# An x load written earlier, second places for stick-breaking keys and values, one dense place less, and other transfer constants in the planner

## The chip, the cores and the metric

One core of a Trainium2 chip runs the whole layer. The metric is the time of one execution on the device in microseconds (us); the figure for a kernel is the median of several executions.

## What is computed

One decoder layer on x of 2048 tokens by 1024 features: RMSNorm, one projection to queries, keys and values for two groups of heads, the two kinds of attention, an output projection with residual, RMSNorm, an MLP with squared ReLU (1024 to 4096 and back) with residual, and a last RMSNorm. Four heads are differential heads (two softmax maps with a distance bias, the second subtracted with weight lam), eight are stick-breaking heads (weights from a running product of 1 - sigmoid):

```python
def diff_attn_block(q1, q2, k1, k2, v, lam, slopes, q0):
    ...
    a = probs(q1, k1) - lam * probs(q2, k2)
    return jnp.einsum('bhqk,bhkd->bhqd', a.astype(v.dtype), v)

def stick_breaking_block(q, k, v, q0):
    ...
    later = lax.cumsum(log_om, axis=3, reverse=True) - log_om
    w = jnp.where(strict, jnp.exp(log_beta + later), 0.0)
    return jnp.einsum('bhqk,bhkd->bhqd', w.astype(v.dtype), v)

def reference(x, attn_norm, w_in, ...):
    h = x
    for l in range(DEPTH):
        a = rmsnorm(h, attn_norm[l])
        h = h + hybrid_mixer(a, w_in[l], ...)
        m = rmsnorm(h, mlp_norm[l])
        u = jnp.square(jax.nn.relu(jnp.einsum('bsd,df->bsf', m, w_up[l])))
        h = h + jnp.einsum('bsf,fd->bsd', u, w_down[l])
    return rmsnorm(h, final_norm)
```

## The kernel before

**Numbers.** Every float32 operand of a matmul is split into two float32r parts, hi (a rounded copy, made by ScalarE) and lo (the rest, a subtraction). A dense product of one 128-wide output slice for one block of 512 tokens is 24 matmuls: 8 chunks of 128 features times hi*hi, hi*lo and lo*hi.

**Blocks and stages.** The tokens stand in reverse order, in four blocks of 512. Block 3 holds the earliest tokens, so it attends to one chunk of keys and block 0 to four. The dense work runs in this order: the projection (QKV) of blocks 3 and 2 together (`emit_qkv((3, 2), ...)`), QKV of blocks 1 and 0, then for each block from 3 to 0 the output projection (`emit_out`) and the MLP (`emit_mlp`). The first use of a weight loads it raw (`split_w`: one transfer of 512 KB), splits it and stores the parts to DRAM; later uses load the parts. In `split_w` the two lo subtractions of a weight run on GpSimd, each as two instructions of 256 columns.

**Three streams and a planner.** The program writes units of work (one instruction, or up to eight matmuls) into three streams: "dense", "diff" (differential heads) and "sb" (stick-breaking heads). `Plan.order` then simulates the five engines with constants for durations and decides one order for all; the engines execute that order as it stands, each its own instructions in turn, and wait by semaphores. Loads and stores are all issued by SyncE (SP), in that order too. TensorE takes a ready unit of an attention head before one of the dense stream (`key`), so dense work fills what the heads leave. For a transfer the planner reckons with 0.42 us on SP, then bytes at a rate by row length behind the transfers that it already has in flight, and 2.2 us more until the data are there. A dense unit may be at most 100 units (`AHEAD`) ahead of the oldest one that isn't placed.

**Places.** Buffers come from pools of slots ("places"). A tile names a home, and a home may use certain pools; tiles of one home and one stream get their places strictly in the order in which the program writes them (`queue`, by `line`): while the first in the line has not been reached, none behind it gets a place. The pools that matter here: "early" (25 places of 4 KB a partition) in the first QKV; "xp" (24 places) during the whole kernel, of which 17 are for "bx", the normed x of blocks 1 and 0; "late" (24 places) opens when the attention is over; the attention's own pools open when all of "early" is done, with one place for the queries of each kind (`qa`, `sq`), two for `ka` and `v`, and one each for `ska` and `sv`, the keys and values of the stick-breaking heads.

**The start.** The first weight, x of block 3, two more weights, then small constants are loaded; three products of block 3 run, then three of block 2 with the same weights. `load_x(2)` is written after the first product, as step 1 of `emit_qkv`, and `norm_to(2)` (scaling by the gain, split to hi on ScalarE and lo on VectorE) as step 2. The tile `rows` of `space`, in which the rows of 1/rms of blocks 3 and 2 stand, has the home "be", as the x tiles have; it is first written when the rms of block 3 is known (`rms_row`, a ScalarE copy from PSUM). The constants' scratch tile `tmp` is a "be" tile too, with the four lambda vectors loaded into it.

Of the kernel before, what the change touches and what calls it, by code (L numbers as in the profile page):

```python
# [28 lines left out]
P = 128  # L29
S = 2048  # L30
D = 1024
# [75 lines left out]
class Plan:  # L107
# [52 lines left out]
    def duration(self, eng, method, kw, out, ins, u):  # L160
        n = math.prod(out.shape[1:])
        small = [v for v in ins if math.prod(v.shape[1:]) * 4 > n]
        sb = [v for v in small if v.tile.home != "psum"]
        if eng == "PE":
            if kw.get("lhsT", kw.get("in_")).dtype == F32:
                return 0.11 if "in_" in kw else 0.225
            return max(0.06, n * 0.000437 + 0.008)
        if eng == "DVE":
            u.dual = len(sb) > 1
            u.psum = any(v.tile.home == "psum" for v in ins)  # L170
            if method == "tensor_tensor_scan":
                return 0.15 + n * 0.0022
            if method == "tensor_reduce":
                n = math.prod(ins[0].shape[1:])
            if method == "tensor_copy" and sb and n >= 256:
                u.dual = True
                return 0.43
            extra = 0.055 if isinstance(kw.get("scalar"), View) else 0.085 if "accum_out" in kw else 0.0
            return 0.15 + n / 960 + extra
        if eng == "ACT":  # L180
            u.psum = any(v.tile.home == "psum" for v in ins)
            extra = 0.09 if isinstance(kw.get("scale"), View) or isinstance(kw.get("bias"), View) else 0.0
            return 0.18 + (0.0 if u.psum else 0.03) + n / 1200 + extra + (0.19 if "accum_out" in kw else 0.0)
        if eng == "POOL":
            if method == "memset":
                return 0.2 + n / 1000
            if kw.get("op") == ALU.pow:
                return 1.65
            u.dual = True
            if method == "tensor_tensor":  # L190
                return 0.19 + n * (0.00216 if out.dtype == F32R else 0.00165)
            if method == "affine_select":
                return 0.3
            return 0.19 + n * 0.00085
        row = min([out.shape[-1]] + [v.shape[-1] for v in ins])
        u.bytes = math.prod(out.shape) * 4
        u.moves = u.bytes / {P: 265e3, HW: 300e3, BW: 335e3, D: 360e3}.get(row, 200e3)
        return 0.42


    def order(self, slots, phase_of, caps, log=None):
# [101 lines left out]
        while done < len(units):  # L303
# [14 lines left out]
            while progress:  # L318
                progress = False
                for e in avail:  # L320
# [3 lines left out]
                    for u in waiting[e]:  # L324
                        if u.ready > now + 1e-9:
                            continue
                        k = self.key(u, now)
                        if best is not None and k >= best[0]:
                            continue
                        if u.stream == "dense" and u.i > dense[at_dense].i + self.AHEAD:  # L330
                            continue
                        spots, ok = [], True
                        for t in u.allocs:
                            if queue[u.stream, self.line(t)][-1] is not t:
                                ok = False
                                break
                            s = place(t, now)
                            if s is None:
                                ok = False
                                break  # L340
                            spots.append((t, s))
                            if len(u.allocs) > 1:
                                free[s[0]].remove(s[1])
                        if len(u.allocs) > 1:
                            for t, s in spots:
                                free[s[0]].append(s[1])
                        if ok:
                            best = k, u, spots
# [16 lines left out]
                    if e == "SP":  # L365
                        avail[e] = now + u.dur
                        begin = max(now + 0.1, dma_free)
                        dma_free = begin + u.moves
                        finish = begin + 2.2 + u.moves
                    else:  # L370
                        finish = start + u.dur
                        avail[e] = finish
                        if e == "PE":
                            if now > self.pe_end + 0.05:
                                gaps.append((now - self.pe_end, now, u))
                            self.pe_end = finish
# [13 lines left out]
                    for s in u.succ:  # L390
                        s.ndeps -= 1
                        s.ready = max(s.ready, finish if s.eng == e else res + (0.04 if s.eng == "POOL" else 0.0))
                        if not s.ndeps:
                            waiting[s.eng].append(s)
                            heapq.heappush(events, s.ready)
                            if s.eng == "PE":
                                heapq.heappush(events, s.ready + self.MARGIN)
                    for t in users.get(id(u), ()):
                        t.left -= 1
                        for kind in gate.get(t.home, ()):  # L400
# [15 lines left out]
        self.report = dict(end=max(u.finish for u in units), busy=busy, gaps=gaps)  # L416
        return out

    MARGIN, AHEAD, pe_end = 0.4, 100, 0.0

    MOST = {("be", "xp"): 7, ("we", "early"): 8, ("xe", "early"): 4, ("w", "xp"): 6, ("x", "xp"): 2, ("y", "xp"): 6,
            ("wm", "xp"): 4, ("wq", "xp"): 5, ("xm", "xp"): 2, ("ym", "xp"): 6, ("x", "late"): 4, ("w", "late"): 12}
# [9 lines left out]
    def key(self, u, now):  # L432
        if u.eng == "PE":
            late = u.ready + self.MARGIN > now
            return (late, u.stream == "dense", u.frac if u.stream != "dense" else u.n)
        if u.eng == "SP":
            return (u.stream == "dense", u.frac if u.stream != "dense" else u.n)

        return u.ready - (10.0 if u.psum else 0.0)

# [11 lines left out]
def layer_kernel(ctx: ExitStack, tc: tile.TileContext, a: dict, out: bass.AP):  # L452
# [5 lines left out]
    tiny = ctx.enter_context(tc.tile_pool(name="tiny", bufs=1))  # L458


    ATT = dict(qa=1, ka=2, e=12, v=2, ha0=2, ha1=2, fa=3, sq=1, ska=1, sv=1, set=8, ser=2, hb0=2, hb1=2, fb=2, osb=1)
    TINY = dict(rvx=2, rrx=2, rx=4, rvh=2, rrh=2, negm=2, l=2, gam=2, rl=2, mm=2, left=8)
    homes = {"be": ["early", "xp"], "we": ["early"], "ye": ["early"], "xe": ["early"], "e": ["e", "e2"], "bx": ["xp"], "b": ["late", "xp"], "w": ["late", "xp"], "y": ["late", "xp"],
             "x": ["late", "xp"], "wm": ["xp"], "ym": ["m", "xp"], "xm": ["xp"], "yq": ["m", "xp"], "wq": ["xp"]}
    homes.update({k: [k] for k in [*ATT, *TINY] if k not in homes})
    plan = Plan(homes)
# [70 lines left out]
    def split_w(name, *at):  # L537

        tiles = [buf(F32R, kind=1) for _ in range(2)]
        if (name, at) in kept:  # L540
            for t, d in zip(tiles, kept[name, at]):
                dma(t, d)
            return Weights(tiles)
        raw = buf(kind=3)
        dma(raw, a[name][at])
        kept[name, at] = []
        for j, t in enumerate(tiles):
            r, hi, lo = raw[:, j * BW:(j + 1) * BW], t[:, 0:BW], t[:, BW:D]
            act.activation(out=hi, in_=r, func=ACTF.Copy)

            for i in range(0, BW, HW):
                pool.tensor_tensor(out=lo[:, i:i + HW], in0=r[:, i:i + HW], in1=hi[:, i:i + HW].bitcast(F32), op=ALU.subtract)
            kept[name, at].append(dt(f"d_{name}_{'_'.join(map(str, at))}_{j}", [P, D]))
            dma(kept[name, at][j], t)
        return Weights(tiles)
# [9 lines left out]
    def halves(last=False):  # L565
# [1 line left out]
        b_ = [buf(F32R, last) for _ in range(KD)]  # L567
        h = [t.rearrange("p (k s) -> p k s", k=2) for t in b_]
        h = h[0::2], h[1::2]
        return h, ([h[0][k // 2][:, k % 2] for k in range(KD)], [h[1][k // 2][:, k % 2] for k in range(KD)], b_)  # L570

    def x_pair():
        t = buf(F32R, kind=2)
# [9 lines left out]

    def space(last=False):
        n = len(rows) % 2
        rows.append(rows[-1] if n else buf(last=last))
        return halves(last) + (rows[-1][:, n * BW:(n + 1) * BW],)

    rows = []
# [1 line left out]
    def norm_x(xs, where):  # L591

        tiles, views, row = where
        for kp, x in enumerate(xs):
            for k in range(2):
                g = g_attn[:, 2 * kp + k:2 * kp + k + 1]
                x_, hi, lo = x[:, k * BW:(k + 1) * BW], tiles[0][kp][:, k], tiles[1][kp][:, k]
                act.activation(out=hi, in_=x_, func=ACTF.Copy, scale=g)
                vec.scalar_tensor_tensor(out=lo, in0=x_, scalar=g, in1=hi.bitcast(F32), op0=ALU.mult, op1=ALU.subtract)
        return views + ([], lambda: rms(xs, row))  # L600
# [427 lines left out]
    for e in starts[1:]:  # L1028
        ws[e] = [split_w("w_qk", e)]

    nxt = {}

    def load_to(b):
        def f():
# [24 lines left out]
    for i, n in enumerate(("lambda_q1", "lambda_k1", "lambda_q2", "lambda_k2")):  # L1059
# [16 lines left out]
    vec.tensor_scalar(out=neglam, in0=neglam, scalar1=-LAM_INIT, scalar2=None, op0=ALU.add)  # L1076


    emit_qkv((3, 2), xs, 3, {1: load_to(2), 2: norm_to(2, False), 12: load_to(1), 13: norm_to(1, True),
                             16: load_to(0), 18: norm_to(0, True)}, ws)  # L1080
    home[:] = ["b", "wq", "yq", "xm"]
    emit_attention(3)
# [4 lines left out]
    def mlp_of(b, xs):  # L1087
        def early():
# [11 lines left out]
    emit_mlp(0, *emit_out(0, xs), 8, lambda: None)  # L1100


    slots = dict(xp=[f"b{i}" for i in range(24)], early=[f"e{i}" for i in range(25)], late=[f"l{i}" for i in range(24)],
                 psum=[f"p{i}" for i in range(8)])
    slots.update({k: [f"{k}{i}" for i in range(n)] for k, n in [*ATT.items(), *TINY.items()]})
    slots.update(m=["m0", "m1"], e2=[f"f{i}" for i in range(4)])
    phases = {k: ["be", "we", "ye", "xe"] for k in [*ATT, "m"]}
    phases.update(e2=["yq", "ym"], late=list(ATT))

    def caps(kind, plan):  # L1110
# [78 lines left out]
```

## Time and profile before

| what | value |
|---|---|
| median of the runs | 2978.68 us (2973.56 to 2979.01, 3 runs) |
| profiled execution, its own time | 2972.79 us |
| its span, first to last instruction | 2971.0 us |
| TensorE busy | 2892.6 us, 97% |
| VectorE, ScalarE, GpSimd busy | 59%, 39%, 37% |
| mean granted TensorE clock | 0.991 |
| DMA: mean rate, share of the 16 engines | 226 GB/s, 67.5% |

A page of the profile gives one execution. Nearly all instructions carry the line of the helper that issues them (L447), so groups are told apart by tile names: `d` and `dn` are the PSUM tiles of dense products, `s`, `pt`, `od` and `os` those of the attention, `w` a split weight, `x` a raw one, `b` a large dense tile, `y` the tile of an output that is to be stored, names with `d_` DRAM. A wait is put down to the event that came last before the waiting instruction began.

### The profile page before, as it was taken

The page shows a single profiled execution, that of the slowest core. Times are in us where ns is not written, and L with a number is a line of the kernel's source. Part 1 is how long each engine was busy: PE and PEld are TensorE (multiplying, and loading weights), DVE is VectorE, ACT ScalarE, POOL GpSimd, SP SyncE. Part 2 cuts the span into 40 slices and gives each one's busy share as a digit, 9 for nine tenths or more (in the row PEclk, how much of TensorE's full clock was granted, in tenths as well). Part 3 has the DMA queues.
Part 4 walks back from the last instruction along what each step waited for, and adds up shares of the span by engine and source line. Part 5 has one row for each costly group of instructions (what it writes and reads, how often), then busy time and mean ns, then how long its engine had stood idle before and what let it go on. Part 6 is the DMA issues. An engine that isn't in the chain of part 4 may idle for free.

```text
span 2971.0 us, 42391 instructions
## 1 busy us (share of the span) xinstructions
PE 2892.6 (97%) x14928; PEld 2439.6 (82%) x14928; DVE 1767.4 (59%) x3193; ACT 1146.2 (39%) x2390; POOL 1099.7 (37%) x1589
## 2 busy tenths in 40 slices
PE   8999999999999999999999999999999999999997
PEld 6889789888887888788788888888888888888886
DVE  5243477777777888884588888887443333421112
ACT  4232255555655555663355555553120100211101
POOL 3221266554677787775344444543000000000000
PEclk9999999999999999999999999999999999999998
DMA  8776897777887877678866665654865556645551
GB/s 268 246 245 202 259 270 233 218 218 230 264 269 244 262 255 254 238 250 288 308 216 204 198 189 192 215 186 169 325 244 200 183 184 241 255 143 205 205 185 71
DMA packets 304164, 670.51 MB, mean 226 GB/s; under 512 B 26960, under 2 KB 121424, under 8 KB 303952
## 3 DMA queue, kind: packets, MB, share of 16 engines
q1 hardware_dynamic: 303952, 667.80, 67.5%
q8 instruction: 119, 1.95, 0.3%
q14 instruction: 93, 0.76, 0.1%
HBM read 491.53 MB, written 176.16 MB: 225 GB/s over the span
## 4 chain that ended last, share of the span: by engine, by line
PE 88%; DMA 6%; DVE 2%; POOL 1%; issue 1%; ACT 1%; SPq 1%; POOLq 0%; DVEq 0%; ACTq 0%
PE d L447 43%; PE dn L447 23%; PE s L447 8%; PE pt L447 6%; PE os L447 4%; PE od L447 3%; DMA v<-d_dv 2%; DMA sq<-d_sq 1%; DMA b<-x_T 1%; SPq L447 1%; DMA qa<-d_dq 1%; DVE b L447 1%; PE r L447 0%; POOL set L447 0%; POOL w L447 0%
## 5 line engine op out<-in xcount | busy, mean ns | idle before, releaser
L447 PE MATMUL d<-b,w 128*128 128x512 f32 x5376 | 1300.9, 395 | 14.1 <-ACT b L447 11.7
L447 PEld LDWEIGHTS d<-b,w 128*128 128x128 f32 x5376 | 1005.3, 189 | 233.1 <-ACT b L447 12.3
L447 PE MATMUL dn<-y,w 128*128 128x512 f32 x3072 | 742.3, 394 | 1.5 <-DVE y L447 1.4
L447 PEld LDWEIGHTS dn<-y,w 128*128 128x128 f32 x3072 | 572.9, 188 | 129.1 <-DVE y L447 1.7
L447 DVE TENSOR_TENSOR b<-b,dn 128x512 f32<-128x512 f32 x416 | 284.8, 685 | 294.9 <-PE dn L447 289.7
L447 POOL TENSOR_TENSOR w<-x,w 128x256 fp32r<-128x256 f32 x384 | 321.8, 860 | 254.5 <-ACT w L447 190.0
L447 POOL TENSOR_TENSOR set<-ser 128x512 f32<-128x512 f32 (+2 forms) x320 | 308.4, 965 | 153.3 <-DVE ser L447 139.7
L447 POOL TENSOR_TENSOR rrx<-rvx,mhalf 128x4 f32<-128x4 f32 x12 | 13.0, 1085 | 880.6 <-DVE rvx L447 880.6
L447 ACT ACTIVATE d<-d 128x512 f32<-128x512 f32 x128 | 74.9, 585 | 596.2 <-DVE d L447 595.8
L447 DVE SCALAR_TENSOR_TENSOR d<-d,b 128x512 f32<-128x512 f32 x128 | 89.3, 698 | 345.8 <-PE d L447 338.2
L447 DVE TENSOR_TENSOR_SCAN ser<-set,left 128x512 f32<-128x512 f32 x192 | 271.8, 1419 | 4.1 <-POOL set L447 3.0
L447 ACT ACTIVATE e<-e,negm 128x512 f32<-128x512 f32 (+3 forms) x320 | 210.5, 658 | 144.3 <-DVE negm L447 134.2
L447 ACT ACTIVATE hb<-pt 128x512 fp32r<-128x512 f32 (+1 forms) x320 | 163.7, 533 | 228.4 <-PE pt L447 135.9
L447 DVE TENSOR_TENSOR hb<-pt,hb 128x512 fp32r<-128x512 f32 (+1 forms) x320 | 186.6, 603 | 54.1 <-ACT hb L447 49.7
L447 DVE CUSTOM_DVE_ANT_0 e<-s,bias 128x512 f32<-128x512 f32 (+3 forms) x320 | 191.4, 598 | 39.4 <-PE s L447 38.9
L447 POOL TENSOR_SCALAR set<-set 128x512 f32<-128x512 f32 (+1 forms) x160 | 120.5, 754 | 240.6 <-ACT set L447 240.2
L447 ACT ACTIVATE set<-s 128x512 f32<-128x512 f32 (+1 forms) x320 | 165.5, 535 | 106.4 <-PE s L447 87.7
L447 PE MATMUL d<-w,b 128*128 128x256 f32 x1536 | 200.9, 285 | 3.3 <-DVE y L447 1.7
L447 PEld LDWEIGHTS d<-w,b 128*128 128x128 f32 x1536 | 190.5, 190 | 8.8 <-DVE y L447 5.1
L447 PE MATMUL s<-ka,qa 128*128 128x512 f32 (+3 forms) x640 | 178.5, 377 | 17.3 <-issue 8.2
L447 PE MATMUL os<-hb,sv 128*128 128x512 f32 (+3 forms) x640 | 186.3, 373 | 5.0 <-DVE hb L447 3.9
L447 PE MATMUL s<-ska,sq 128*128 128x512 f32 (+3 forms) x640 | 181.6, 379 | 7.6 <-DMA sq<-d_sq 3.8
(91 smaller groups left out, 3037.5 us busy)
## 6 DMA issues: line engine op xcount, KB each, us to landing
w<-d_w_up SPq DMA_DIRECT2D x192, 512.0 KB, 5.5
w<-d_w_down SPq DMA_DIRECT2D x192, 512.0 KB, 5.0
ka<-d_dk SPq DMA_DIRECT2D x80, 512.0 KB, 5.4
v<-d_dv SPq DMA_DIRECT2D x144, 256.0 KB, 4.3
d_w_up<-w SPq DMA_DIRECT2D x64, 512.0 KB, 5.4
d_w_down<-w SPq DMA_DIRECT2D x64, 512.0 KB, 6.2
w<-d_w_out SPq DMA_DIRECT2D x48, 512.0 KB, 6.9
ska<-d_sk SPq DMA_DIRECT2D x80, 256.0 KB, 4.1
```

The source lines that it names most:

```text
L447: fn(*[v.ap() if isinstance(v, View) else v for v in args], **{k: v.ap() if isinstance(v, View) else v for k, v in kw.items()})
```

## The change

Seven edits, all in the planner and in what is written into it:

1. The planner counts a transfer as 0.48 us on SP instead of 0.42, at rates 6 to 11% lower, and with 2.6 us instead of 2.2 until the data are there.
2. `ska` and `sv` have two places each instead of one (2 KB a partition each), and "xp" has 23 instead of 24 (4 KB).
3. `load_x(2)` is written right behind the first three weights, ahead of the constants, instead of at step 1 of `emit_qkv`.
4. The `rows` tile of blocks 3 and 2 has a home of its own, "re", in the pool "early".
5. In the first QKV a weight's lo part is one VectorE instruction of 512 columns instead of two GpSimd instructions of 256.
6. The parts of a normed x are named by column ranges, so that the planner lets a product depend on the half that it reads.
7. Constants `STORE`, `LOAD` and `EARLY` come in, with values (0, 0 and 100) at which their conditions do as before.

```diff
-        u.moves = u.bytes / {P: 265e3, HW: 300e3, BW: 335e3, D: 360e3}.get(row, 200e3)
-        return 0.42
+        u.moves = u.bytes / {P: 250e3, HW: 270e3, BW: 300e3, D: 320e3}.get(row, 200e3)
+        return 0.48
...
+                        if e == "SP" and u.out.home is None and now < u.ready + self.STORE:
+                            continue
...
-                        if u.stream == "dense" and u.i > dense[at_dense].i + self.AHEAD:
+                        if u.stream == "dense" and u.i > dense[at_dense].i + (self.AHEAD if len(self.seen) > 1 else self.EARLY):
...
-                        finish = begin + 2.2 + u.moves
+                        finish = begin + 2.6 + u.moves
...
-    MARGIN, AHEAD, pe_end = 0.4, 100, 0.0
+    MARGIN, AHEAD, pe_end, STORE, LOAD, EARLY = 0.4, 100, 0.0, 0.0, 0.0, 100
...
-            return (u.stream == "dense", u.frac if u.stream != "dense" else u.n)
+            return (u.ready + self.LOAD > now, u.stream == "dense", u.frac if u.stream != "dense" else u.n)
...
-    ATT = dict(qa=1, ka=2, e=12, v=2, ha0=2, ha1=2, fa=3, sq=1, ska=1, sv=1, set=8, ser=2, hb0=2, hb1=2, fb=2, osb=1)
+    ATT = dict(qa=1, ka=2, e=12, v=2, ha0=2, ha1=2, fa=3, sq=1, ska=2, sv=2, set=8, ser=2, hb0=2, hb1=2, fb=2, osb=1)
...
-            for i in range(0, BW, HW):
-                pool.tensor_tensor(out=lo[:, i:i + HW], in0=r[:, i:i + HW], in1=hi[:, i:i + HW].bitcast(F32), op=ALU.subtract)
+            for i in range(0, BW, BW if home[0] == "be" else HW):
+                c = slice(i, i + (BW if home[0] == "be" else HW))
+                (vec if home[0] == "be" else pool).tensor_tensor(out=lo[:, c], in0=r[:, c], in1=hi[:, c].bitcast(F32),
+                                                                 op=ALU.subtract)
...
-        return h, ([h[0][k // 2][:, k % 2] for k in range(KD)], [h[1][k // 2][:, k % 2] for k in range(KD)], b_)
+        return h, tuple([b_[2 * (k // 2) + j][:, k % 2 * BW:(k % 2 + 1) * BW] for k in range(KD)] for j in range(2)) + (b_,)
...
-        rows.append(rows[-1] if n else buf(last=last))
+        rows.append(rows[-1] if n else buf(last=last) if last else tile_view("re", [P, D], F32, "b"))
...
-    nxt = {}
+    nxt = {2: load_x(2)}
...
-    emit_qkv((3, 2), xs, 3, {1: load_to(2), 2: norm_to(2, False), 12: load_to(1), 13: norm_to(1, True),
+    emit_qkv((3, 2), xs, 3, {2: norm_to(2, False), 12: load_to(1), 13: norm_to(1, True),
...
-    slots = dict(xp=[f"b{i}" for i in range(24)], early=[f"e{i}" for i in range(25)], late=[f"l{i}" for i in range(24)],
+    slots = dict(xp=[f"b{i}" for i in range(23)], early=[f"e{i}" for i in range(25)], late=[f"l{i}" for i in range(24)],
...
-    phases = {k: ["be", "we", "ye", "xe"] for k in [*ATT, "m"]}
+    phases = {k: ["be", "we", "ye", "xe", "re"] for k in [*ATT, "m"]}
```

## Rows read from the trace of the kernel before

**Rows 1.** Busy time by engine over the whole span (the profile's page).

```profile
PE 2892.6 (97%) x14928; PEld 2439.6 (82%) x14928; DVE 1767.4 (59%) x3193; ACT 1146.2 (39%) x2390; POOL 1099.7 (37%) x1589
```

**Rows 2.** Stretches by stage: width, busy per engine, PEclk, DMA share, GB/s.

```profile
0.00:300.00 300.00, 284.21 (x1582) 244.99 (x1583) 110.00 (x159) 100.20 (x165) 84.81 (x110) 0.98 0.73 241
300.00:820.00 520.00, 498.23 (x3072) 440.79 (x3071) 368.87 (x783) 263.63 (x631) 271.41 (x437) 0.99 0.81 242
...
960.00:1470.00 510.00, 500.27 (x2549) 418.51 (x2549) 384.75 (x686) 267.07 (x567) 352.07 (x491) 1.00 0.79 266
...
1500.00:2080.00 580.00, 573.75 (x3088) 486.66 (x3086) 487.05 (x912) 304.39 (x656) 267.05 (x394) 0.99 0.60 192
2080.00:2600.00 520.00, 520.00 (x2281) 424.86 (x2281) 209.50 (x310) 72.59 (x109) 6.58 (x6) 1.00 0.63 233
```

**Rows 3.** Waits of TensorE, 300 to 2080 us: in total, times, longest.

```profile
PE s L447 <- issue: 8.2, 3, 5.5
PE s L447 <- DMA qa<-d_dq: 7.2, 4, 3.9
PE od L447 <- DMA v<-d_dv: 6.9, 9, 1.7
...
PE s L447 <- DMA sq<-d_sq: 3.8, 4, 1.6
PE s L447 <- DMA d_dk<-y: 3.0, 2, 1.7
...
PE s L447 <- DMA ska<-d_sk: 1.4, 2, 0.8
```

**Rows 4.** Timeline of the start; in brackets idle time before, and its releaser.

```profile
24.54 3.02 SPq L447 DMA_DIRECT2D b<-x_T  x4
...
29.23 0.20 ACT L447 ACTIVATE lexp<-lsum 128x2 f32<-128x2 f32 x1 [11.19 <-DVE lsum L447]
29.34 0.58 ACT L447 ACTIVATE b<-r 128x512 f32<-128x512 f32 x1
...
33.45 3.77 ACT L447 ACTIVATE b<-b,g_attn 128x512 fp32r<-128x512 f32 x6
...
34.20 0.80 PE L447 MATMUL d<-b,w 128*128 128x512 f32 x1 [4.55 <-ACT b L447]
```

**Rows 5.** Stretches of 4 us in the start; columns as in rows 2.

```profile
28.00:32.00 4.00, 1.66 (x8) 1.01 (x6) 2.94 (x8) 1.99 (x5) 0.00 (x0) 1.00 0.99 405
32.00:36.00 4.00, 1.28 (x2) 0.77 (x3) 3.45 (x5) 4.00 (x8) 2.90 (x3) 0.71 1.00 383
36.00:40.00 4.00, 3.37 (x8) 2.17 (x8) 3.59 (x5) 3.44 (x5) 1.19 (x2) 0.50 0.91 247
40.00:44.00 4.00, 4.00 (x11) 3.03 (x10) 2.33 (x4) 1.95 (x3) 0.00 (x0) 0.51 0.97 270
```

**Rows 6.** The chain that ended last, two pieces from 14 to 29 us.

```profile
15.26 7.09 POOL w L447 x6
...
22.73 5.83 DMA b<-lambda_k
```

**Rows 7.** Instruction groups, 0 to 300 us: busy, mean ns, idle before.

```profile
L447 POOL TENSOR_TENSOR w<-x,w 128x256 fp32r<-128x256 f32 x96 | 80.2, 868 | 171.7 <-ACT w L447 123.3 <-DVE y L447 29.1 <-DMA d_dq<-y 10.7
...
L447 DVE TENSOR_TENSOR y<-y 128x512 fp32r<-128x512 f32 x32 | 23.9, 756 | 18.5 <-ACT y L447 18.4
```

**Rows 8.** Transfers of one kind: number, KB each, median us to landing.

```profile
sq<-d_sq SPq DMA_DIRECT2D x64, 256.0 KB, 5.9
```

**Rows 9.** Timeline around 900 us, two rows.

```profile
896.49 0.58 SPq L447 DMA_DIRECT2D qa<-d_dq  x1
...
904.12 2.04 PE L447 MATMUL s<-ka,qa 128*128 128x512 f32 x4 [5.47 <-issue]
```

**Rows 10.** What SP waited for, 300 to 820 us: total, times, longest.

```profile
SPq L447 <- PE s L447: 93.4, 42, 8.7
SPq L447 <- DVE y L447: 57.8, 16, 15.0
```

More of the change, by code (lines that the diff above doesn't have):

```diff
@@ L397, in order @@
                                 heapq.heappush(events, s.ready + self.MARGIN)
+                            if s.eng == "SP":
+                                heapq.heappush(events, s.ready + self.STORE)
+                                heapq.heappush(events, s.ready + self.LOAD)
                     for t in users.get(id(u), ()):
@@ L458, in layer_kernel @@
     tiny = ctx.enter_context(tc.tile_pool(name="tiny", bufs=1))
-    ATT = dict(qa=1, ka=2, e=12, v=2, ha0=2, ha1=2, fa=3, sq=1, ska=1, sv=1, set=8, ser=2, hb0=2, hb1=2, fb=2, osb=1)
+    ATT = dict(qa=1, ka=2, e=12, v=2, ha0=2, ha1=2, fa=3, sq=1, ska=2, sv=2, set=8, ser=2, hb0=2, hb1=2, fb=2, osb=1)
     TINY = dict(rvx=2, rrx=2, rx=4, rvh=2, rrh=2, negm=2, l=2, gam=2, rl=2, mm=2, left=8)
-    homes = {"be": ["early", "xp"], "we": ["early"], "ye": ["early"], "xe": ["early"], "e": ["e", "e2"], "bx": ["xp"], "b": ["late", "xp"], "w": ["late", "xp"], "y": ["late", "xp"],
+    homes = {"re": ["early"], "be": ["early", "xp"], "we": ["early"], "ye": ["early"], "xe": ["early"], "e": ["e", "e2"], "bx": ["xp"], "b": ["late", "xp"], "w": ["late", "xp"], "y": ["late", "xp"],
              "x": ["late", "xp"], "wm": ["xp"], "ym": ["m", "xp"], "xm": ["xp"], "yq": ["m", "xp"], "wq": ["xp"]}
@@ L596, in norm_x @@
                 g = g_attn[:, 2 * kp + k:2 * kp + k + 1]
-                x_, hi, lo = x[:, k * BW:(k + 1) * BW], tiles[0][kp][:, k], tiles[1][kp][:, k]
+                x_, hi, lo = x[:, k * BW:(k + 1) * BW], views[0][2 * kp + k], views[1][2 * kp + k]
                 act.activation(out=hi, in_=x_, func=ACTF.Copy, scale=g)
```

## The prediction

> **What bounds the kernel now.** I read four views in turn: the busy times of the engines, the stretches by stage, TensorE's waits, and the timeline of the start. TensorE is busy 97% of the span and no other engine reaches 60% [rows 1], so the time is TensorE's work plus what it idles plus what it loses at the lower clock. The change removes no matmul, so it can only touch the last two. The stages show where these lie [rows 2]: 15.8 us idle in the first 300 us, 21.8 from 300 to 820 (second QKV beside the attention of blocks 3 and 2), 9.7 from 960 to 1470, 6.3 from 1500 to 2080, and none from 2080 to 2600, where dense work runs alone. The granted clock of 0.99 in the stages that begin at 300 and at 1500 is another 5.2 and 5.8 us. So some 70 us can be won at all, and nothing behind 2080.
>
> What ends the waits between 300 and 2080 us is mostly a transfer [rows 3]: queries 7.2 and 3.8 us, values of differential heads 6.9, a store on which a key load hangs 3.0, `ska` only 1.4. I add the 8.2 of "issue": its longest wait (5.5 us) ended at 904.1 us before a product with the queries that were loaded from 896.5 us on [rows 9], 7.6 us earlier, so it looks like one more late transfer. That makes 30.5 us in 24 waits, 1.3 us each.
>
> **The change part by part.**
>
> *The earlier x load with the `rows` tile's own home.* Before, x of block 2 is issued at 24.5 us, and TensorE idles 4.55 us until ScalarE has made the first hi part of it at 34.2 [rows 4]. Why so late: the places of "be" tiles are given in written order, and `rows` stood ahead of x(2) in that line; it gets its place when the planner reaches the copy of the row (the ScalarE copy from `r`), which really ran at 29.34: ScalarE had first waited 11.19 us for the exponential of the lambda vectors, whose last transfer stands in the chain with 5.83 us [rows 4, 6]. With `rows` in "re" and the load written earlier, x(2) waits only for the places of the eight parts of block 3, given when its norm runs, a good ten us earlier by the order of the program. The 11.19 us that ScalarE idles before 29.23 have room for the split of x(2).
>
> What is at stake: from 28 to 40 us TensorE idles 2.34 + 2.72 + 0.63 = 5.7 us. Then it works at a granted clock near 0.50 to 44 us, the lower of the two levels (1.2 GHz): half of 1.28 + 3.37 + 4.00 us of busy time, 4.3 us, is lost [rows 5]. Together 10.0. I take 8: the three products of block 2 will still be fed piece by piece by ScalarE and VectorE, as those of block 3 are. Bounds 0 (the load comes earlier, but something else on ScalarE holds the split) and 10.
>
> The Trainium skill, "TensorE: Matmul & The Clock Gate", section "HAM oscillation — how this bites in real kernels", says that a wait for a transfer can send the clock to half, so that the next work starts slowly. The trace agrees: 0.71, 0.50, 0.51 behind the stall. By idle time alone this term would be at most 5.7.
>
> *lo parts on VectorE.* In the first QKV 96 GpSimd instructions of 868 ns (80.2 us busy) become 48 on VectorE. The nearest row, a subtraction of two SBUF operands of 512 columns, is 756 ns [rows 7], so VectorE gains 36.3 us and stands at 146 of 300 us. Neither engine ends a wait of note there. At the start six GpSimd instructions stand in the chain for 7.09 us [rows 6]; two weights would take VectorE 4 x 0.756 = 3.0 us, so the stores that wait for them, and with them everything behind on SP, leave earlier. This helps the term above and is not counted again. Bounds: gain 1; loss 1.5, if two such instructions get in front of the lo parts of x that TensorE waits for. I take 0; the cover is that VectorE is only half busy.
>
> *The slower transfer in the planner.* A 256 KB load in rows of 256 columns was 0.1 + 2.2 + 0.87 = 3.2 us and is now 0.1 + 2.6 + 0.97 = 3.7, plus more behind a full queue. The trace has 5.9 for `sq` [rows 8], so the planner still expects data early, but by 0.5 us less. No instruction becomes faster; the order changes, so that the consumer of a load stands later, behind other TensorE work. If each of the 22 waits that aren't for `ska` got shorter by 0.5 us, that is 11 us. But it is a new order of everything, with late operands in other places, so I take half, 5.5. Bounds 11 gained and 6 lost (the same half with the sign turned). Work that was placed on the assumption of a free SP moves by 0.06 us an issue; against SP's waits for tiles [rows 10] I cost that at nothing.
>
> *Second places for `ska` and `sv`.* The next chunk's keys and values can be loaded while the last one's are in use. TensorE waited 1.4 us for keys [rows 3]; I take 1.4 gained, bounds 0 and 3 (with the second query load issued sooner). `sq` and `qa` keep one place and stay what is late next: SP waits 93.4 us for `s` products to release such tiles in 300 to 820 us [rows 10].
>
> *The clock.* From 300 to 2080 the shown stages lose 5.2 + 5.8 = 11.0 us to the clock beside 37.8 idle; 6.9 us of waits less gives 6.9 / 37.8 x 11.0 = 2 back. Bounds 0 and 4.
>
> *One place less in "xp".* While x of blocks 1 and 0 holds 17 places, 7 were left for weights and outputs of the second QKV; now 6. That stage already idles 21.8 us [rows 2], and SP waits 57.8 us, up to 15 in one go, for outputs `y` to store [rows 10]. If its idle time went with the inverse of the places, one of seven costs 21.8 / 7 = 3.1. I take 3, bounds 0 (attention fills the hole) and 22 (the idle time doubles). The first QKV's tiles may hold seven places too, and 7 + 17 is more than 23, so the last part of x(0) may have to wait for the end of the first QKV; that is two subtractions, 1.5 us at 756 ns, against two products of block 1 that go first, so nothing.
>
> *The column ranges and the three new constants* change the planner's dependencies slightly or not at all: nothing.
>
> Sum: -8 - 5.5 - 1.4 - 2 + 3 = -13.9 us. The profiled execution took 2972.8 us (1.8 around its span), so it would take 2958.9. The median of the runs is 5.9 above it; against that, 2964.8 us.
>
> **The rivals.**
>
> *A. The order gains fully.* All the planner's steps work: 10 at the start, 11 + 3 of waits, 4 of clock, nothing for the place: -28, 2951. For it speaks that transfers end most of the waits; against it that qa and sq still land two us later than planned.
>
> *B. New late places for old.* Only the start gains (8), the lost place takes 3 and the rest is redrawn: -5, 2974, within the measure. For it: waits of 1.3 us are spread over the whole stage, with no one place that the change mends.
>
> *C. The start does not gain.* x(2) lies early, but ScalarE's next instruction is the exponential for lam, which waits for lambda loads that now stand behind x(2) in the "be" line; the split of x(2) is queued behind it, TensorE waits as before. Or the x(2) issues stand on SP behind a store that waits for a split. Then -13.9 + 8 = -6, 2973, on the edge. The trace shows such a halt of ScalarE now [rows 4, 6]. On the second form the Trainium skill, "DMA: Bandwidth & Descriptors", section "Anatomy of one DMA — SWDGE (gpsimd) path", says that a semaphore wait happens on the issuing sequencer, which would delay everything behind; the stores of the first weights here do so.
>
> *D. Slower: the lost place.* In 300 to 820 us the second QKV can't prefetch its weights and drain its outputs at once; dense work is then missing as a filler while each short head of block 3 waits for its queries. Its idle time and its loss to the clock double, +21.8 and +5.2; with the 8 of the start and 6.9 of waits off, that is +12, 2991. It decides from the point where that stage's idle time grows by 13.9 + 3 = 17 us. Against it: none of the long waits of TensorE there is for a dense weight [rows 3].
>
> **How the numbers follow.** Forecast 0.48, A 0.12, B 0.15, C 0.10, D 0.15. A difference under 0.2% (6 us) can't be told from none. Faster: forecast, A and half of C, 0.65. Same: B and half of C, 0.20. Slower: D, 0.15. Range: it must leave out no more than 2 in 10. Below, 2942 takes in A and the 5 us by which the lowest run lies under the median; above, 2981 takes in B and C and the mildest of D. What is left out is most of D and a little at the lower end.
>
> **What would show it.** Right: x of block 2 issued before 16 us, no idle stretch over 1 us on TensorE between 16 and 60 us, granted clock 1.00 from 28 to 44; TensorE's transfer waits between 300 and 2080 us near 23 us rather than 30, none for `ska`; GpSimd 80 us less and VectorE 36 us more busy than before in the first 300. Wrong: a stall of 4 us or more at 25 to 45 us (C), as many transfer waits as before (B), or over 35 us idle from 300 to 820 (D).

## The result, and the profile after

The median fell from 2976.12 (four runs; three of them gave the 2978.68 that stands ahead of the prediction) to 2935.55 us: ratio 0.9865, 95% interval 0.9844 to 0.9885, so 40 us less where 14 were forecast, and below the range that was given. The profiled execution took 2937.48 us.

The page of the changed kernel, busy times and the row of the granted clock:

```profile
span 2935.7 us, 42296 instructions
...
PE 2880.7 (98%) x14928; PEld 2433.8 (83%) x14928; DVE 1803.2 (61%) x3241; ACT 1145.3 (39%) x2390; POOL 1035.3 (35%) x1493
...
PEclk9999999999999999999999999999999999999999
```

The same 14928 matmuls. TensorE's idle time went from 2971.0 - 2892.6 = 78.4 to 2935.7 - 2880.7 = 55.0 us, 23.4 less; its busy time fell by 11.9 us, because the mean granted clock rose from 0.991 to 0.995. The two together are the 35.3 us of the span: a third of the gain is clock.

The start of the changed kernel, timeline (releaser of an idle time in brackets), then stretches of 4 us with the columns of [rows 2]:

```profile
14.58 1.77 SPq L452 DMA_DIRECT2D b<-x_T  x4
...
20.75 1.98 ACT L452 ACTIVATE b<-b,g_attn 128x512 fp32r<-128x512 f32 x3 [3.27 <-DMA b<-x_T]
...
28.48 9.52 PE L452 MATMUL d<-b,w 128*128 128x512 f32 x40
```

```profile
28.00:32.00 4.00, 4.00 (x21) 3.29 (x20) 4.00 (x6) 3.15 (x6) 0.00 (x0) 1.00 0.17 51
32.00:36.00 4.00, 4.00 (x19) 3.21 (x18) 4.00 (x7) 1.21 (x3) 0.00 (x0) 1.00 0.10 24
36.00:40.00 4.00, 4.00 (x23) 3.43 (x22) 1.05 (x6) 0.20 (x1) 0.94 (x1) 1.00 0.91 263
40.00:44.00 4.00, 4.00 (x21) 3.28 (x20) 2.10 (x5) 1.76 (x3) 0.07 (x1) 1.00 0.96 306
```

x of block 2 is issued at 14.6 instead of 24.5 us [rows 4], TensorE doesn't stop, the clock stays at 1.00, and 84 matmuls begin in these 16 us instead of 29 [rows 5].

Behind the start, the stages and TensorE's waits from 300 to 2080 us, longest first:

```profile
0.00:300.00 300.00, 289.29 (x1629) 251.16 (x1630) 130.94 (x211) 101.31 (x167) 4.79 (x15) 1.00 0.74 251
300.00:820.00 520.00, 508.71 (x3125) 451.04 (x3124) 381.83 (x787) 270.65 (x643) 289.48 (x447) 0.99 0.81 249
820.00:960.00 140.00, 130.17 (x685) 107.13 (x684) 123.03 (x221) 84.87 (x182) 113.22 (x149) 0.99 0.75 245
960.00:1470.00 510.00, 504.55 (x2566) 422.65 (x2565) 384.66 (x689) 269.23 (x564) 346.07 (x484) 1.00 0.79 271
...
1500.00:2080.00 580.00, 579.02 (x3095) 491.93 (x3093) 485.57 (x893) 291.81 (x629) 261.66 (x375) 1.00 0.61 199
```

```profile
PE s L452 <- DMA qa<-d_dq: 6.5, 6, 2.0
PE os L452 <- DVE hb L452: 4.7, 7, 2.0
PE pt L452 <- DVE fb L452: 4.1, 1, 4.1
PE pt L452 <- POOL set L452: 3.7, 3, 1.6
...
```

Of the transfers only the queries of differential heads are left, 6.5 us, where [rows 3] showed 30.5. No other row of the list names a transfer: the waits for `v`, `sq`, `ska`, the store, and those of "issue" are gone. What takes the head of the list are waits for VectorE and GpSimd of the kind that was there before; all that isn't transfers or "issue" sums to 21.5 us, where it was 15.0.

### The profile page after: what moved, and what is told of

Read it like the earlier page. It is cut to its first block, busy times and chain, and to the rows that moved or that the text cites. A ratio compares the mean times of both kernels' runs of the same rounds, so it can differ in the third digit from the quotient of the medians.

```text
span 2935.7 us, 42296 instructions
## 1 busy us (share of the span) xinstructions
PE 2880.7 (98%) x14928; PEld 2433.8 (83%) x14928; DVE 1803.2 (61%) x3241; ACT 1145.3 (39%) x2390; POOL 1035.3 (35%) x1493
## 4 chain that ended last, share of the span: by engine, by line
PE 92%; DMA 3%; DVE 2%; issue 1%; ACT 1%; POOL 1%; SPq 0%; POOLq 0%; DVEq 0%; ACTq 0%
PE d L452 45%; PE dn L452 24%; PE s L452 8%; PE pt L452 7%; PE os L452 4%; PE od L452 3%; DMA qa<-d_dq 1%; DVE b L452 1%; PE r L452 0%; SPq L452 0%; POOL set L452 0%; DVE y L452 0%; ACT y L452 0%; DVE e L452 0%; DMA x<-w_out 0%
## 5 line engine op out<-in xcount | busy, mean ns | idle before, releaser
L452 POOL TENSOR_TENSOR w<-x,w 128x256 fp32r<-128x256 f32 x288 | 241.4, 856 | 68.0 <-ACT w L452 59.8
L452 PE MATMUL s<-ska,sq 128*128 128x512 f32 (+3 forms) x640 | 174.4, 371 | 0.9 <-PE os L452 0.7
```

Of the source, the lines that this page charges most:

```text
L452: fn(*[v.ap() if isinstance(v, View) else v for v in args], **{k: v.ap() if isinstance(v, View) else v for k, v in kw.items()})
```

## The experiments

Eighteen runs. "Waits" is what TensorE waited for transfers (with "issue") from 300 to 2080 us in the profiled execution, all its rows summed; the same sum is 31.6 us for the kernel before (26 waits; the rows shown ahead of the prediction make 30.5 of them) and 6.5 for the changed one. Ratios are to the kernel before on the same chip. The profiled execution need not be a middle one: that of `b_issue`, 2962.2 us, is the fastest of its ten. The column ranges and the three new constants (edits 6 and 7) were not taken out alone.

| run | what it is | median us | ratio (95%) | waits us |
|---|---|---|---|---|
| b_const | before + constants | 2943.1 | 0.9897 (0.9882-0.9912) | 6.6 |
| b_xload | before + early x, `rows` home | 2968.9 | 0.9977 (0.9961-0.9993) | 23.6 |
| b_dve | before + VectorE splits | 2976.7 | 1.0005 (0.9989-1.0021) | 27.6 |
| b_places_re | before + places, `rows` home | 2951.1 | 0.9927 (0.9903-0.9951) | 18.2 |
| b_re | before + `rows` home | 2971.6 | 0.9991 (0.9977-1.0005) | 30.4 |
| b_rate | before + rates alone | 2964.0 | 0.9949 (0.9931-0.9968) | 24.0 |
| b_lat | before + 2.6 us alone | 2960.6 | 0.9935 (0.9917-0.9952) | 20.8 |
| b_issue | before + 0.48 us alone | 2975.8 | 0.9990 (0.9970-1.0010) | 24.9 |
| b_const_att | constants, attention only | 2965.0 | 0.9964 (0.9947-0.9981) | 25.8 |
| b_const_dense | constants, dense only | 2973.5 | 0.9994 (0.9975-1.0013) | 27.6 |
| b_const_re | constants + `rows` home | 2941.7 | 0.9892 (0.9867-0.9916) | 6.7 |
| a_noconst | changed, old constants | 2961.0 | 0.9936 (0.9915-0.9957) | 19.2 |
| a_half | changed, half the step | 2947.3 | 0.9908 (0.9881-0.9935) | 17.5 |
| a_more | changed, constants further | 2961.3 | 0.9955 (0.9940-0.9969) | 12.6 |
| a_noplaces | changed, old places | 2939.4 | 0.9881 (0.9865-0.9896) | 3.9 |
| a_only23 | changed, one place, 23 in xp | 2935.9 | 0.9870 (0.9854-0.9886) | 6.0 |
| a_nodve | changed, GpSimd splits | 2953.9 | 0.9932 (0.9914-0.9951) | 21.4 |
| a_noxload | changed, old x load and home | 2939.3 | 0.9881 (0.9858-0.9903) | 6.9 |

### One edit alone in the kernel before

`b_const` takes the two hunks of the diff with the rates, 0.48 and 2.6; `b_dve` the `split_w` hunk; the other two:

```diff
+    homes = {"re": ["early"], "be": ["early", "xp"],
...
+        rows.append(rows[-1] if n else buf(last=last) if last else tile_view("re", [P, D], F32, "b"))
...
-    nxt = {}
+    nxt = {2: load_x(2)}
```

```diff
+    homes = {"re": ["early"], "be": ["early", "xp"],
...
+        rows.append(rows[-1] if n else buf(last=last) if last else tile_view("re", [P, D], F32, "b"))
...
-    ATT = dict(... sq=1, ska=1, sv=1, ...)
+    ATT = dict(... sq=1, ska=2, sv=2, ...)
...
-    slots = dict(xp=[f"b{i}" for i in range(24)], ...)
+    slots = dict(xp=[f"b{i}" for i in range(23)], ...)
```

> The kernel before with only the slower transfer constants in the planner. Theory (the prediction's terms): 5 to 8 us less, ratio near 0.998, the start unchanged (idle 4.5 us at 34 us stays). Rival (the constants carry what the forecast missed): 20 to 30 us less, all of it between 300 and 2080 us, with transfer waits of TensorE down from 30 us to under 12.

> The kernel before with only the earlier x load and the rows tile's own home. Theory (the prediction's terms): the stall at 28 to 44 us goes and nothing else changes on average: 8 to 11 us less, ratio 0.997 to 0.996, and TensorE's transfer waits from 300 us on stay near 30 us. Rival 1 (a new order moves the time by chance): anything from 20 us less to 10 us more, with a change behind 300 us that is as large as that of the start. Rival 2 (the rows tile's home also lets the first QKV end in a better state for the attention, so the stage from 300 to 400 us gains): 15 to 22 us less, the extra in 300 to 400 us.

> The kernel before with only the lo parts of the first QKV's weights on VectorE. Theory: within 0.2%, 0 to 2 us less at the start (a quicker second weight). Rival (the GpSimd splits held up stores on SP, and these the loads behind them): 5 us or more less, in the first 100 us.

> The kernel before with only the second places for the stick-breaking keys and values, 23 places in xp, and the rows tile's own home (x of block 2 is still loaded where it was). Theory: 1.4 us less for the second places, 3 more for the lost one, so the same within 0.2%, if the home alone does not make x of block 2 earlier; if it does, up to 8 less. Rival (second places bring the attention's pace, the forecast's term for them was too small): 10 to 20 us less, between 300 and 1000 us.

The constants alone bring 31 of the 40 us: the forecast's 5.5 was wrong and the rival of this run right (31.6 us against its 20 to 30). TensorE's 26 waits for transfers (with "issue") became 6. With no other edit, the stage that idled 21.8 us idles 3.2 (stages, then waits of TensorE for transfers from 300 to 2080 us, then median us from issue to landing, all of `b_const`):

```profile
300.00:820.00 520.00, 516.79 (x3163) 457.90 (x3162) 379.00 (x782) 273.42 (x643) 288.67 (x448) 1.00 0.84 257
```

```profile
PE os L447 <- DMA sv<-d_sv: 2.2, 1, 2.2
PE s L447 <- DMA qa<-d_dq: 2.2, 1, 2.2
...
PE s L447 <- DMA sq<-d_sq: 1.0, 2, 0.5
...
PE s L447 <- DMA ska<-d_sk: 1.0, 1, 1.0
```

```profile
qa<-d_dq SPq DMA_DIRECT2D x64, 256.0 KB, 5.5
sq<-d_sq SPq DMA_DIRECT2D x64, 256.0 KB, 5.8
```

The transfers are hardly faster: `sq` lands after 5.8 us as against 5.9 [rows 8]; in the changed kernel its median is 6.7, and TensorE doesn't wait for it. What changed is what stands between the issue of a load and the first product that reads it: over the 128 loads of queries (`qa` and `sq`) that time has a median of 10.2 us before, 11.6 in `b_const` and 11.7 in the changed kernel (worked out from the traces, for each load up to the next product with its tile). The stall at the start (2.6 us idle from 28 to 32) is still there in this run, as it should be.

The VectorE splits alone are worth nothing that can be measured, as forecast. The early x gives 0.2%, its interval just reaching what can be told from none: 5.8 us, less than the 8 to 11 that were expected of it. The places with the home gave 0.7% here, more than the -1.4 + 3 us plus 8 of the forecast; what is theirs in the changed kernel is another matter (below).

### Which of the constants

`b_rate`, `b_lat` and `b_issue` change one of the three numbers; `b_const_att` and `b_const_dense` all of them for one kind of stream:

```diff
-        u.moves = u.bytes / {P: 265e3, HW: 300e3, BW: 335e3, D: 360e3}.get(row, 200e3)
-        return 0.42
+        slow = u.stream != "dense"
+        rates = {P: 250e3, HW: 270e3, BW: 300e3, D: 320e3} if slow else {P: 265e3, HW: 300e3, BW: 335e3, D: 360e3}
+        u.moves = u.bytes / rates.get(row, 200e3)
+        return 0.48 if slow else 0.42
...
-                        finish = begin + 2.2 + u.moves
+                        finish = begin + (2.6 if u.stream != "dense" else 2.2) + u.moves
```

> The kernel before with the lower transfer rates in the planner alone (issue time and landing constant as before). All constants together gave 0.9897. Theory Q (the backlog: between 300 and 820 us the DMA engines are full, and rates that are 10% lower add up over the transfers in flight, which a wait of one transfer alone does not show): the rates carry most of it, 18 to 28 us less, idle time of TensorE in 300 to 820 us under 10 us. Theory L (the fixed 0.4 us at landing does it): under 8 us less. Theory R (any new order would do): the same gain as with the others of this set, about 10 us for each.

> The kernel before with the landing constant 2.6 instead of 2.2 us alone. Theory Q: 4 to 8 us less (22 waits, 0.4 us each at most, and not all of them). Theory L: 18 to 28 us less, TensorE's transfer waits from 300 us on under 12 us. Theory R: about 10 us less, as the others of this set.

> The kernel before with 0.48 instead of 0.42 us for an issue on SP alone. Theories Q and L: within 0.2% of before. Theory S (SP itself is the bottleneck of the start of loads, and the planner must know it): 10 us less or more. Theory R: about 10 us less.

> The kernel before with the slower transfer constants for the transfers of attention heads alone. Theory (a load's own lateness is what TensorE waits for): most of the 31 us, 18 us less or more. Rival (the backlog is: dense loads and stores make up most of the bytes in the queue, so it is theirs that must be counted slower): under 10 us less.

> The kernel before with the slower transfer constants for the dense stream's transfers alone. Theory (a load's own lateness): under 10 us less. Rival (the backlog of the dense transfers): 18 us less or more. If both are needed, this run and the one with the attention's transfers each give 8 to 16 us.

Rates 13 us, landing constant 16, issue time nothing: between theory Q and theory L, and the two parts nearly add up to the whole. Theory R (any new order would do) falls by `b_issue`, `b_dve` and `b_const_dense`, which are new orders too and stay at before. But single orders with the old constants lie between 2951 and 2977 us (below), and `b_rate`, `b_lat` and `b_const_att` lie within that, so what each part of the constants is worth is not shown. In `b_lat` the median from issue to first product is 10.2 us, as before, though it is 16 us faster. Split by stream, the attention's own transfers give 11 us and the dense ones nothing, but together 31. My reading, argued and not shown, is that a head's load is late by its own landing time and by what is queued ahead of it, and that the planner has to know both. The 11 us are less than the "most of it" that was expected for the attention alone.

### How far to go

```diff
-        u.moves = u.bytes / {P: 250e3, HW: 270e3, BW: 300e3, D: 320e3}.get(row, 200e3)
-        return 0.48
+        u.moves = u.bytes / {P: 235e3, HW: 240e3, BW: 265e3, D: 280e3}.get(row, 200e3)
+        return 0.54
...
-                        finish = begin + 2.6 + u.moves
+                        finish = begin + 3.0 + u.moves
```

> The changed kernel with the transfer constants half way between before and changed: 0.45 us an issue, rates 257, 285, 317 and 340, 2.4 us to landing. Constants of before gave 2961 us in this kernel, the changed ones 2936. If the time follows the constants smoothly (each tenth of a us shortens waits): 2944 to 2954. If there is a threshold that half of the step does not reach, 2956 to 2963; if half is enough, 2934 to 2942. If each order is a throw of its own, anywhere from 2930 to 2965 without a relation.

> The changed kernel with transfers still slower in the planner: 0.54 us an issue, rates 235, 240, 265 and 280, 3.0 us to landing. If the gain comes from consumers standing far enough behind their loads, and 6.5 us of transfer waits are left: 0 to 8 us less than the changed kernel, 2928 to 2936. If the constants of the changed kernel are about right and more makes the planner idle or crowd its other engines: 0 to 15 us more. If the gain was the luck of one order: 10 us or more slower.

> The changed kernel with the transfer constants of before. If the constants are what carries the middle of the kernel (theories Q and L): 20 to 30 us slower than the changed kernel, so 2956 to 2966, with the start still without its stall. If the second places or the earlier x do it as well (the edits overlap): under 12 us slower than the changed kernel, so 2936 to 2948.

In the changed kernel the old constants give 2961, half the step 2947, the whole 2936, a further step 2961. The first three lie on a line, as the smooth theory has it, but inside the 2930 to 2965 of chance as well. The fourth turns back, 25 us above the changed kernel, which is outside the first two expectations and inside the third, the luck of one order. Its query loads do stand further ahead of their first product, 15.1 us in the median where the changed kernel has 11.7, and yet its transfer waits are 12.6 us. Of its waits one place can be shown, the change from the MLP of block 3 to the output projection of block 2, in `a_more` (stretches of 20 us, and the largest piece of the chain just before):

```profile
1450.00:1470.00 20.00, 15.29 (x71) 12.43 (x70) 18.12 (x34) 11.09 (x22) 12.73 (x15) 0.83 0.64 186
1470.00:1490.00 20.00, 15.32 (x70) 12.35 (x69) 20.00 (x26) 5.15 (x10) 12.70 (x13) 0.91 0.63 224
```

```profile
1410.97 8.73 DMA x<-w_down
```

The changed kernel idles 1.2 and 1.6 us in these two stretches, this one 4.7 each, at a lower clock. As I read it, the last raw weights come late there and dense work is short as a filler; no run shows that. That it is the further step as such, and not this one order, was not tried a second time.

### The home of the rows tile, and edits undone in the changed kernel

`b_re` is `b_xload` without the moved load; `b_const_re` adds the constants to it. `a_only23` keeps 23 places in "xp" and takes the second places away:

```diff
-    ATT = dict(... sq=1, ska=2, sv=2, ...)
+    ATT = dict(... sq=1, ska=1, sv=1, ...)
```

`a_noplaces` puts back this line and the 24 places, `a_nodve` the `split_w` hunk, `a_noxload` the five hunks with `re`, `load_x(2)` and `load_to(2)`.

> The kernel before with only the rows tile's own home; x of block 2 is loaded where it was written before. Theory (the line of the be tiles was what held x of block 2): the load is issued before 20 us and the stall at 28 to 44 us is gone, 6 to 11 us less at 50 us of work, ratio 0.996 to 0.998; the earlier place of the load in the program is then worth nothing. Rival (the place in the program decides): x of block 2 still at 24 us, stall as before, ratio 1.000.

> The kernel before with the slower transfer constants and the rows tile's own home, and nothing else. If these two are the whole change: 2934 to 2941, ratio 0.986 to 0.989, transfer waits of TensorE from 300 us on under 10 us and no stall at the start. If the second places, the written place of the load or the VectorE splits still carry a part: 2943 or more.

> The changed kernel with one place each for the stick-breaking keys and values and 24 places in xp, as before. Theory (the forecast's terms, -1.4 and +3): within 0.2% of the changed kernel, 2930 to 2942, ratio to before 0.986 to 0.989. Rival (the second places bring what places and home gave together, some 12 us beyond the start): 2945 to 2952, ratio near 0.991.

> The changed kernel with 23 places in xp but one place each for the stick-breaking keys and values: the price of the lost place alone, against the run with 24 and one each. Theory: 3 us slower than that one, so within 0.2% of it. Rival (the lost place was dear and the second places paid for it): 8 us or more slower than the run with 24, with more idle time of TensorE from 300 to 820 us. Rival (the lost place costs nothing): equal within the spread.

> The changed kernel with the weights' lo parts of the first QKV on GpSimd again. Theory: within 0.2% of the changed kernel (2930 to 2941), the first 300 us as short as with VectorE. Rival (the last 6 us between the changed kernel and the one with constants and home alone come from these splits): 2941 us or more.

> The changed kernel with the rows tile again in the line of the be tiles and x of block 2 loaded at its old place. The start must show the stall again: about 7 to 11 us more lost by 60 us than in the changed kernel. Theory A (what the start gains stays): 2943 to 2947. Theory B (most of it is given back between 300 and 1000 us, as in the kernel before with the home alone): 2935 to 2941.

The issue of x of block 2 in `b_re` (timeline), and its stage from 300 us on:

```profile
14.87 2.80 SPq L447 DMA_DIRECT2D b<-x_T  x4
```

```profile
300.00:820.00 520.00, 496.20 (x3046) 439.72 (x3045) 372.62 (x777) 260.76 (x629) 274.35 (x432) 0.99 0.79 239
```

The home alone brings the load to 14.9 us: the line of the "be" tiles was the cause, and the written place adds next to nothing (14.4 us in `b_xload`, which has both). The stall is gone (4.00 us busy in each stretch of 4 us from 28 to 44). Yet the whole is only 1.9 us faster, within the measure; the stage from 300 us idles 23.8 us instead of 21.8. In the changed kernel, putting home and load back costs 3.8 us (there the stall is shorter, 3.5 us more idle time in the first 300). So of the 8 to 10 us of the start 1.9 and 5.8 arrive at the end in the kernel before, each with an uncertainty of some 4 us. Whether the attention's order gives it back by its nature or the two orders did so by chance stays open.

With the constants, the home alone comes to 2941.7 (`b_const_re`), between its two expectations; the 6 us between it and the changed kernel are not clear of the intervals.

The two edits of places together are worth 3.8 us in the changed kernel (2939.4 to 2935.6). The second places alone are worth 0.3 (2935.9 to 2935.6, both with 23 places), and the lost place cost nothing: with one place each, 23 places took 3.5 us less than 24 (2935.9 and 2939.4, on one chip). None of this is clear of the spread. Beside the old constants the places and the home gave 23, the home alone 2. That would fit with both edits, places and constants, curing the same waits, so that their gains don't add; but it is one order, and chance of that size isn't excluded.

`a_nodve` is 18 us slower than the changed kernel: not within 0.2%, and three times the 6 us that its rival had to explain. It isn't the first QKV, which idles 9.6 us in 300 as against 10.7. From 820 to 960 us it idles as long as the changed kernel, at a granted clock of 0.95 where that has 0.99; from 960 to 1470 it idles 12.7 us where that idles 5.4. Its two long waits there, at 886 and 1078 us, are for queries, where GpSimd and VectorE split as they do in the changed kernel (stages, then timeline of `a_nodve`):

```profile
0.00:300.00 300.00, 290.43 (x1628) 252.25 (x1629) 112.35 (x163) 101.33 (x167) 84.20 (x111) 1.00 0.74 250
...
820.00:960.00 140.00, 130.25 (x670) 108.61 (x669) 113.49 (x208) 82.06 (x175) 103.60 (x141) 0.95 0.72 236
960.00:1470.00 510.00, 497.27 (x2525) 416.40 (x2524) 376.37 (x670) 265.08 (x557) 344.36 (x478) 1.00 0.78 264
```

```profile
886.20 2.07 PE L452 MATMUL s<-ka,qa 128*128 128x512 f32 x4 [4.88 <-DMA qa<-d_dq]
```

```profile
1078.30 0.71 PE L452 MATMUL s<-ka,qa 128*128 128x256 f32 x4 [3.74 <-DMA qa<-d_dq]
```

Its transfer waits are 21.4 us, back at the level of the old constants. So one order of those with the changed constants was an unlucky one. With the changed constants seven orders were run: 2936, 2936, 2939, 2939, 2942, 2943 and 2954; with the old ones, before and five others without the constants' parts: 2951 to 2977. Three pairs of kernels differ in all the constants and in nothing else: before and `b_const`, `b_re` and `b_const_re`, `a_noconst` and the changed kernel. The constants are worth 31.6, 29.9 and 25.4 us in them, and the transfer waits fall by 25.0, 23.7 and 12.7 us. Orders with the constants left alone were off by some 20 us at most (`b_places_re` and `a_nodve`), so one pair would not settle it; three that agree show the constants as a whole to be the cause of most of the gain. Over all runs the time goes with the transfer waits: up to 7 us of them, 2936 to 2943; 17 to 32, 2947 to 2977; `a_more` stands between them in waits, 12.6, with 2961. From `b_const` to before that is 31 us of time for 25 us of waits, while the mean granted clock falls from 0.995 to 0.991.

## Why the prediction was wrong

Right: what bounds the kernel, the stage, the sign, and that transfers end most of the waits. The start is as described, step by step: `rows` held the line, the load at 14.6 us, no stall, clock 1.00 from 28 to 44. The splits as such: GpSimd 80 us less busy in the first 300 us (84.81 to 4.79), VectorE 21 more where 36 were said.

The step that failed is "The slower transfer in the planner": "If each of the 22 waits that aren't for `ska` got shorter by 0.5 us, that is 11 us. But it is a new order of everything, with late operands in other places, so I take half, 5.5." The mechanism was right, consumers that stand later, and the size was not. Measured: transfer waits down by 25 us (`b_const`), time by 31. Two things were wrong in it. Each wait was to get shorter by the 0.5 us that one isolated transfer is now counted longer, although the same paragraph says "plus more behind a full queue". The consumers of queries moved by 1.4 us in the median (10.2 to 11.6), and 20 of 26 waits went altogether. Whether it is the queue that makes the 0.5 into 1.4 stays open: `b_rate` (13 us) and `b_const_att` (11 of 31) fit with it, but neither is clear of what one order can do. And the halving had no row behind it: new orders do put late operands elsewhere, but one that reckons with later data also leaves fewer of them, and the bound "11" was no bound. The term "2" for the clock was too small for the same reason, since it was worked out from 6.9 us of waits: of the 11.9 us less busy time some 4 belong to the start by the prediction's own reckoning, and the other 7 or so are above its bound of 4.

The "-8" of the start was right at the start (with the home alone 1630 matmuls have begun by 300 us instead of 1582, some 9 us of work at that pace) and about 4 at the end. The "+3" for the lost place was nothing (and by its own rule, the inverse of the places, seven to six would be 21.8 / 6 = 3.6), and the "-1.4" for the second places measured 0.3; neither can be told from the spread. All the other edits together brought 7.5 us on top of the constants (2943.1 to 2935.6, on two chips; 9.5 by the ratios), where the start, the second places and the lost one were put at 6.4, so the miss lies in the constants and their clock. Rival A ("the order gains fully", 2951) named the right case and was cut off by the same bound; D did not come, the stage from 300 to 820 idles 11.3 us instead of 21.8. The range's lower end hung on A's bounds.

The Trainium skill's page "TensorE: Matmul & The Clock Gate", section "HAM oscillation — how this bites in real kernels", says that waits can cost twice, in idle time and in clock: that holds over the whole kernel, 23.4 us of idle time and 11.9 of busy time at unchanged work.

## What to carry to other kernels

Where an order is planned ahead and executed as it stands, an operand's landing time in the plan is a lever of its own: compare it with the median in the profile's list of transfers. Too little showed here as many waits of about 1 us for loads that are spread over a stage. The median isn't the value to put in, though: the step from 3.2 to 3.7 us for a 256 KB load gained, well below the 5.8 to 5.9 that the trace has for queries, and the next step, to 0.1 + 3.0 + 1.09 = 4.2, lost 25 us in the one order that was run. One order more or less is worth 5 to 20 us in a kernel like this, so judge an edit by several orders, or by the waits that it should remove, before its time is believed.

## What the runs showed of the hardware

VectorE's instructions of two SBUF operands got quicker when GpSimd left the first QKV. Groups of the changed kernel, 0 to 300 us, then one of the kernel before:

```profile
L452 DVE TENSOR_TENSOR w<-x,w 128x512 fp32r<-128x512 f32 x48 | 31.6, 687 | 15.1 <-ACT w L452 14.9
...
L452 DVE SCALAR_TENSOR_TENSOR b<-b,g_attn 128x512 fp32r<-128x512 f32 x32 | 22.6, 746 | 3.7 <-ACT b L452 3.3
L452 DVE TENSOR_TENSOR y<-y 128x512 fp32r<-128x512 f32 x33 | 22.5, 691 | 12.3 <-ACT y L452 11.4
L452 DVE SCALAR_TENSOR_TENSOR y<-d,b 128x512 f32<-128x512 f32 x33 | 22.5, 691 | 64.0 <-PE d L452 60.4 <-ACT b L452 1.7 <-DMA d_dk<-y 1.3
```

```profile
L447 DVE SCALAR_TENSOR_TENSOR y<-d,b 128x512 f32<-128x512 f32 x32 | 21.8, 690 | 69.3 <-PE d L447 62.2 <-DMA d_w_qk<-w 3.5 <-ACT b L447 3.3
```

The `y` subtraction took 756 ns beside GpSimd [rows 7] and takes 691 without it, the gain and subtraction of x (`b<-b,g_attn`) 898 and 746, and the moved split 687 where 756 were reckoned. That is most of why VectorE gained 21 us of busy time and not 36. `y<-d,b`, of whose two inputs one lies in PSUM, stayed as it was, 690 and 691. Two runs that move only the splits show the same: `b_dve` takes the `y` subtraction from 756 to 691, and `a_nodve` from 691 back to 749. The Trainium skill, "SBUF — State Buffer", section "Who interferes with whom", says that a VectorE instruction with two SBUF inputs contends with a GpSimd instruction that reads SBUF. These rows agree with it; that it is this contention, and not another effect of the moved work, is not shown.
